# RWKV finish pair by pair with small root tiles, and memory attention's first loads moved into the chunk loop

## The chip, the cores and the metric

One core of one Trainium2 chip runs the whole layer in one launch. The metric is the device time of an execution in microseconds (us). The engines are TensorE (PE), VectorE (DVE), ScalarE (ACT), GpSimd (POOL) and SyncE (SP); SP's queue issues most DMAs.

## The reference, cut to what matters

A decoder layer in float32: a SwiGLU half-step, a mixer of three branches, merged by sigmoid gates and projected, and another SwiGLU half-step; D_MODEL 1024, 1024 tokens. The parts that the change touches:

```python
def rwkv7_mix(p, ...):                      # first branch
    ...
    y = rwkv7_recurrence(r, decay, k, v, -kk, kk * a)   # 8 heads of 64, token by token
    mean = jnp.mean(y, axis=-1, keepdims=True)
    var = jnp.mean(jnp.square(y - mean), axis=-1, keepdims=True)
    y = ((y - mean) * lax.rsqrt(var + RWKV_GN_EPS) * gn_g + gn_b)
    y = y + jnp.sum(r * k * r_k, axis=-1, keepdims=True) * v
    return (y.reshape(B, S, RWKV_WIDTH) * g)            # g = sigmoid(gd) @ g_up

def memory_cross_attention(q, mem_n, w_kv):             # 4 heads of 128, 256 memory tokens
    km, vm = jnp.split(mem_n @ w_kv, 2, axis=-1)
    ...
    s = jnp.einsum('bshd,bmhd->bhsm', q * MEM_HEAD_DIM ** -0.5, km)
    pr = jax.nn.softmax(s, axis=-1)
    o = jnp.einsum('bhsm,bmhd->bshd', pr, vm)

merged = g_a * (y_a @ w_branch[0]) + g_b * (y_b @ w_branch[1]) + g_c * (y_c @ w_branch[2])
```

## The kernel before

Activations lie feature-major: 128 features on the partitions, tokens along the free side. Float32 products are made of three matmuls of 128x128 weights against 512 tokens, out of high and low parts (`mm3`); `operand` splits each weight block on ScalarE (`w_hi`, L300) and VectorE (`w_lo`, L302), ahead of its use.

A planner builds the instruction order of every engine at compile time from priorities and estimated times; on the chip each engine runs its own list in that order and waits on semaphores. `keep_in_program_order` pins the instructions given to it to their order in the text, each engine's among themselves. `issue_after(x)` puts an instruction behind `x` on `x`'s engine. `high_priority` moves work up. Tiles come from pools; a new tile over old memory waits until the old tile has been read. A pool opened with `reuse_waits="tile"` waits tile by tile; the pool `attw` of the attention's small tiles isn't opened so.

The order in the middle of the mixer:

1. `rwkv_chain` runs the recurrence in 16 chunks of 64 tokens; `chunk_fetch` loads the next chunk's operands (`f`, `dinv`). Each chunk has a serial chain of small matmuls (`z`, `y`, `gram`, `bkt`, all in line L1218 or L1258). Matmuls of the two early gates, 10 and 11 (`pgate`, lines 377 to 379), stand between them.
2. Later gates and two branch products form a generator, `filling`; `fill(n, behind)` takes steps of it until n matmuls are covered, behind a given matmul. Most steps hold 6 matmuls, a gate has 48, and what a step takes beyond n counts for the next call.
3. `rwkv_finish` works on 4 pairs of heads, each in two halves of 512 tokens. Per half: GpSimd squares `y` (`ysq`, L1335), ScalarE squares it rounded (`ysq_hi`, L1336), VectorE takes the difference (`ysq_lo`, L1337), two matmuls sum over a head (`var`, L1347), ScalarE takes Ln (L1349) and, once all halves are through, Exp (L1353) over whole pairs: 1 / sqrt. Then per half three VectorE steps with y, gain, bias, bonus (`bo_in`) and the output gate's product (`gup`, L1369), and a store (L1372). `yrs` is one tile of 16 KB per partition.
4. `gate_out` of a gate ends in Tanh on ScalarE (L1483). While the finish is emitted it goes to a list, `held`, which is worked off between the roots and the final steps.
5. `attention` runs 8 memory blocks and 8 window blocks of 128 queries in a software pipeline: scores of block i+1 (`msc`), filling, values of block i-1, turning of block i (`mptr`), filling. `load` of a memory block fetches the queries, `qm`. The keys `km_in` and values `vm_in` are loaded at the start of the attention's section; their pools lie where those of the chain were.

A function's ScalarE table is loaded when the one that is in doesn't hold it; `preload_act_table_set` asks for the one with both Ln and Exp. PSUM has 8 banks of 512 values: 4 under the tag "mm" (`pgate` among them), 4 under "bg" (`var`, `gup`, `msc` among them).

## Time and profile before

| | |
|---|---|
| median of 3 runs | 2264.32 us (2263.44 to 2266.61) |
| the profiled execution | 2261.35 us, span 2259.3 us |
| TensorE busy | 2229.2 us (99%), granted clock 0.998 |
| VectorE, ScalarE, GpSimd busy | 1641.6, 1032.3, 80.1 us |
| DMA | 432.43 MB, 191 GB/s over the span |

Busy times are sums of instructions on an engine. The profile can say for each idle stretch which instruction or DMA ended it (waits), follow the work that ended last back through its releasers (the chain), and give busy times and the granted clock for any window. The chunk loop stands at about 1061 to 1165 us of the span, the finish at 1171 to 1212, the first memory block at 1224.

### The profile page before, as it was taken

How to read it: one execution, taken by the hardware profiler on the slowest of the kernel's cores; microseconds unless marked ns; L12 is line 12 of the kernel's file. 1: busy time of each engine (PE TensorE's matmuls, PEld its weight loads, DVE VectorE, ACT ScalarE, POOL GpSimd, SP SyncE). 2: the span in 40 equal slices, each digit the busy share in tenths (PEclk: the TensorE clock that was granted, in tenths of full speed). 3: DMA queues.
4: the chain of work that ended last, by engine and by line, in shares of the span. 5: the costliest groups of instructions: out<-in, count | busy, mean ns of one | idle time of the engine just before them, and what ended most of it. 6: DMA issues, size and time to landing. Idle time of an engine off the chain costs nothing.

```text
span 2259.3 us, 34577 instructions
## 1 busy us (share of the span) xinstructions
PE 2229.2 (99%) x12304; PEld 1832.0 (81%) x12304; DVE 1641.6 (73%) x2761; ACT 1032.3 (46%) x1935; POOL 80.1 (4%) x154
## 2 busy tenths in 40 slices
PE   8999999999999999999999999999999999999998
PEld 6888888888887788887877887788888888888887
DVE  6988777766698887863656578794898886656576
ACT  6622333454556654444454454444663223345451
POOL 0000000000000011001330000000000000000000
PEclk9999999999999999999999999999999999999999
DMA  8565566686665456455426887564565653347663
GB/s 284 173 204 170 198 210 215 229 289 213 185 217 185 126 148 212 156 166 182 145 86 238 274 277 253 164 223 138 174 210 179 194 187 103 114 165 249 205 194 122
DMA packets 272237, 432.43 MB, mean 191 GB/s; under 512 B 50848, under 2 KB 89760, under 8 KB 271808
## 3 DMA queue, kind: packets, MB, share of 16 engines
q1 hardware_dynamic: 255968, 402.09, 55.0%
q10 hardware_dynamic: 14816, 27.07, 3.5%
q8 instruction: 97, 1.59, 0.3%
q0 software_dynamic: 1280, 1.05, 0.2%
q14 instruction: 76, 0.62, 0.1%
HBM read 292.75 MB, written 136.31 MB: 190 GB/s over the span
## 4 chain that ended last, share of the span: by engine, by line
PE 90%; DVE 4%; DMA 3%; ACT 2%; issue 1%; SPq 0%; ACTq 0%; DVEq 0%
PE px L377 9%; PE px L379 9%; PE px L378 9%; PE po L377 6%; PE po L378 6%; PE po L379 6%; PE pz L377 4%; PE pz L379 4%; PE pz L378 4%; PE pgate L377 2%; PE pgate L378 2%; PE pgate L379 2%; PE pr L377 2%; PE pr L378 2%; PE pr L379 2%; PE pb L377 2%
## 5 line engine op out<-in xcount | busy, mean ns | idle before, releaser
L300 ACT CAST w_hi<-w_raw 128x512 fp32r<-128x512 f32 x608 | 376.1, 620 | 714.5 <-PE px L378 181.3
L302 DVE TENSOR_TENSOR w_lo<-w_raw,w_hi 128x512 fp32r<-128x512 f32 x608 | 417.1, 688 | 193.2 <-ACT w_hi L300 176.9
L377 PE MATMUL po<-u,w_hi 128*128 128x512 f32 (+1 forms) x476 | 180.9, 380 | 0.0
L379 PE MATMUL po<-u,w_lo 128*128 128x512 f32 (+1 forms) x476 | 180.9, 380 | 0.0
L378 PE MATMUL po<-u,w_hi 128*128 128x512 f32 (+1 forms) x476 | 180.9, 380 | 0.0
L377 PE MATMUL px<-u,w_hi 128*128 128x512 f32 x380 | 148.0, 390 | 0.8 <-DVE km L1611 0.8
L377 PE MATMUL pz<-u,w_hi 128*128 128x512 f32 x380 | 148.1, 390 | 0.0
L379 PE MATMUL px<-u,w_lo 128*128 128x512 f32 x380 | 148.0, 389 | 0.0
L378 PE MATMUL px<-u,w_hi 128*128 128x512 f32 x380 | 147.9, 389 | 0.0
L378 PE MATMUL pz<-u,w_hi 128*128 128x512 f32 x380 | 147.8, 389 | 0.0
L379 PE MATMUL pz<-u,w_lo 128*128 128x512 f32 x380 | 147.8, 389 | 0.0
L377 PE MATMUL px<-f,w_hi 128*128 128x512 f32 x352 | 137.1, 390 | 0.1
L379 PE MATMUL px<-f,w_lo 128*128 128x512 f32 x352 | 137.0, 389 | 0.0
L378 PE MATMUL px<-f,w_hi 128*128 128x512 f32 x352 | 137.0, 389 | 0.0
L486 DVE TENSOR_TENSOR u<-hid,u 128x512 fp32r<-128x512 f32 x114 | 78.4, 690 | 49.9 <-ACT u L485 49.1
L378 PEld LDWEIGHTS po<-u,w_hi 128*128 128x128 f32 x476 | 89.5, 188 | 17.0
L379 PEld LDWEIGHTS po<-u,w_lo 128*128 128x128 f32 x476 | 89.5, 188 | 17.0
L377 PEld LDWEIGHTS po<-u,w_hi 128*128 128x128 f32 x476 | 89.5, 188 | 16.9
L377 PE MATMUL pgate<-u,w_hi 128*128 128x512 f32 x256 | 103.1, 403 | 0.0
L485 ACT CAST u<-hid 128x512 fp32r<-128x512 f32 x114 | 70.7, 620 | 68.8 <-DMA hid<-form_d 59.4
L378 PE MATMUL pgate<-u,w_hi 128*128 128x512 f32 x256 | 101.3, 396 | 0.0
L379 PE MATMUL pgate<-u,w_lo 128*128 128x512 f32 x256 | 100.1, 391 | 0.0
(456 smaller groups left out, 5189.4 us busy)
## 6 DMA issues: line engine op xcount, KB each, us to landing
w_raw<-in_ffn_in SPq DMA_DIRECT2D x224, 256.0 KB
hid<-form_d SPq DMA_DIRECT2D x154, 256.0 KB
w_raw<-in_win SPq DMA_DIRECT2D x112, 256.0 KB
form_d<-g SPq DMA_DIRECT2D x88, 256.0 KB
w_raw<-ffn_sum_d SPq DMA_DIRECT2D x88, 256.0 KB
form_d<-h SPq DMA_DIRECT2D x66, 256.0 KB
w_raw<-in_ffn_out SPq DMA_DIRECT2D x66, 256.0 KB
first_d<-first SPq DMA_DIRECT2D x48, 256.0 KB
```

What stands on the lines that cost most here:

```text
L300: self.nc.scalar.copy(hi, x)
L302: self.split_last = self.nc.vector.tensor_tensor(lo, x, hi.bitcast(F32), ALU.subtract)
L377: mm(out, wh, xh, start=first, stop=False, **kw)
L378: mm(out, wh, xl, start=False, stop=False, **kw)
L379: self.last_mm = mm(out, wl, xh, start=False, stop=last, **kw)
L485: self.nc.scalar.copy(hi, x)
L486: self.nc.vector.tensor_tensor(lo, x, hi.bitcast(F32), ALU.subtract)
```

## The change

Root tiles: `yrs` becomes a tag of three tiles of 2 KB, one for each half, with Ln and Exp one after the other. The finish runs pair by pair: variance, filling of `FINISH[1]`, final steps and stores, filling of `FINISH[2]`; the splits for the output gate stand ahead of it. The held gates come after the finish, behind its last Exp, and gate 11's Tanh is pinned in program order. The filling ahead of the attention is cut. `km_in`, `vm_in` and the queries' tiles get a pool of their own, `ahead`, on the right side of SBUF, open from before the chunk loop to the attention's end; keys, values and the first two blocks' queries are loaded in chunks 3, 5, 7 and 8, behind the chunk's fetch (`asked`).

```diff
+FINISH = (16, 6, 10)
 class WindowBlock(Block):
-        self.qs = self.pool.tile([P, 4, P], F32, tag="qs", name="qs", bufs=2)
+        self.qs = self.ahead.tile([P, 4, P], F32, tag="qs", name="qs", bufs=2)
 class MemoryBlock(Block):
-        self.qm = self.pool.tile([P, 4, P], F32, tag="qs", name="qm", bufs=2)
+        self.qm = self.ahead.tile([P, 4, P], F32, tag="qs", name="qm", bufs=2)
 # chunk_fetch
-            S.dma_start(n["d"][q * 64 : q * 64 + 64], inv_d[c, :, q].rearrange("p s t -> s p t"))
+            self.asked = S.dma_start(n["d"][q * 64 : q * 64 + 64], inv_d[c, :, q].rearrange("p s t -> s p t"))
 # rwkv_chain
             nxt = None if last else load(c + 1)
+            if c in beside:
+                with self.tc.issue_after(self.asked.ins):
+                    beside[c]()
 # rwkv_finish
-        rs = pool.tile([P, NPAIR, T], F32, name="yrs", bufs=1)
-        squares = []
+        squares, rs = [], []
         square(0)
         square(1)
-        self.fill(22, self.behind)
-        for i, (p, cols) in enumerate(halves):
-            ps = self.psum("var")
-            for n, x in enumerate(squares[i]):
-                end = keep(nc.tensor.matmul(ps, self.bones_r, x, start=n == 0, stop=n == 1))
-            square(i + 2)
-            keep(S.activation(rs[:, p, cols], ps, ACT.Ln, bias=self.gn_eps, scale=1.0 / C))
-            if i % 2:
-                self.fill(8 if p < NPAIR - 1 else 30, end)
-        for p in range(NPAIR):
-            keep(S.activation(rs[:, p], rs[:, p], ACT.Exp, scale=-0.5))
         for h in (0, 1):
             self.split(self.sg[:, h * TH : (h + 1) * TH], *(x[:, h * TH : (h + 1) * TH] for x in sg))
         self.split(self.g_up, *up)
+        self.fill(FINISH[0], self.behind)
+        for p in range(NPAIR):
+            for h in (0, 1):
+                cols = halves[h][1]
+                ps = self.psum("var")
+                for n, x in enumerate(squares[2 * p + h]):
+                    end = keep(nc.tensor.matmul(ps, self.bones_r, x, start=n == 0, stop=n == 1))
+                square(2 * p + h + 2)
+                rs.append(pool.tile([P, TH], F32, tag="yrs", name="yrs", bufs=3))
+                keep(S.activation(rs[-1], ps, ACT.Ln, bias=self.gn_eps, scale=1.0 / C))
+                root = keep(S.activation(rs[-1], rs[-1], ACT.Exp, scale=-0.5))
+            self.fill(FINISH[1], end)
+            for h in (0, 1):
+                ...
+                r = rs.pop(0)
+                (the three VectorE steps, gup and the store as before)
+            self.fill(FINISH[2], end)
         held, self.held = self.held, None
-        for f in held:
-            f()
-        (the final steps of all halves, self.fill(10, end) after every second)
+        with self.tc.issue_after(root.ins):
+            for f in held:
+                f()
 # gate_out
-            self.nc.scalar.activation(t[:, h * TH : (h + 1) * TH], ps[h], ACT.Tanh, ...)
+            made = self.nc.scalar.activation(t[:, h * TH : (h + 1) * TH], ps[h], ACT.Tanh, ...)
+            if g == GATES_EARLY - 1:
+                self.tc.keep_in_program_order(made)
 # attention
-        blocks[0].load()
-        blocks[1].load()
-        self.fill(50, self.behind)
 # mixer
+            stay = contextlib.ExitStack()
+            ahead = stay.enter_context(tc.tile_pool(reuse_waits="tile", name="ahead", bufs=1, side="right"))
+            km = ahead.tile([P, 4, MEM], F32, name="km_in")
+            vm = ahead.tile([P, 2, 512], F32, name="vm_in")
+            ...
+            beside = {3: lambda: nc.sync.dma_start(km, km_d), 5: lambda: nc.sync.dma_start(vm, vm_d), 7: blocks[0].load, 8: blocks[1].load}
-                self.fill(12, self.solved[-5])
-                self.fill(8, self.solved[-1])
+                self.fill(8, self.solved)
-                km = ap.tile([P, 4, MEM], F32, name="km_in")
-                vm = ap.tile([P, 2, 512], F32, name="vm_in")
-                nc.sync.dma_start(km, km_d)
-                nc.sync.dma_start(vm, vm_d)
```

## Prediction

> **What bounds the kernel now.** I read the page's busy table first, then the waits, then the chain and the engines' timelines around the places that the diff touches. The table says that TensorE is the bound:

> ```profile
> span 2259.3 us, 34577 instructions
> PE 2229.2 (99%) x12304; PEld 1832.0 (81%) x12304; DVE 1641.6 (73%) x2761; ACT 1032.3 (46%) x1935; POOL 80.1 (4%) x154
> ```

> Only 30.1 us of the span are left in which TensorE is idle. The change adds no matmul and takes none out, so it can win only what idles, or runs slowly, where it works. The waits between 1160 and 1230 us (line, releaser, total, times, longest) give that:

> ```profile
> PE msc L101 <- DMA vm_in<-vm_d: 4.3, 1, 4.3
> PE var L1347 <- ACT ysq_hi L1336: 1.2, 1, 1.2
> PE var L1347 <- DVE ysq_lo L1337: 0.5, 2, 0.3
> SPq L191 <- DMA y_d<-yrs: 3.5, 1, 3.5
> ```

> The long one stands where the attention begins. The timelines of SyncE's queue and TensorE, then two steps of the chain, show why:

> ```profile
> 1206.07 5.63 SPq L1372 DMA_DIRECT2D y_d<-yrs  x4
> 1216.04 0.93 SPq L191 DMA_DIRECT2D qm<-att_d  x2
> 1218.03 0.43 SPq L1830 DMA_DIRECT2D vm_in<-vm_d  x1
> 1224.57 3.46 PE L101 MATMUL msc<-km_in,qm 128*128 128x256 f32 x8 [4.28 <-DMA vm_in<-vm_d]
> ...
> 1218.03 6.46 DMA vm_in<-vm_d
> 1224.57 3.46 PE msc L101 x8
> 1237.60 1.73 PE msc L101 x8
> ```

> The query loads stood behind the last store of `yrs`, whose memory they reuse; km and vm stood behind them; TensorE ran out of filling work and waited 4.28 us. The first eight score matmuls then cost 3.46 us, the next eight 1.73: the clock had dropped.

> ```profile
> 1175.60:1185.30 9.70, 7.93 (x32) 5.74 (x31) 5.64 (x7) 9.19 (x14) 6.33 (x6) 1.00 0.08 27
> 1224.50:1228.00 3.50, 3.43 (x9) 2.84 (x10) 0.69 (x1) 0.00 (x0) 0.00 (x0) 0.56 0.61 231
> ```

> In these windows (width, then busy time of PE, PEld, DVE, ACT and POOL, granted clock, DMA share, GB/s) the clock is 1.00 around the three short waits at `var`, which together are 9.70 - 7.93 = 1.77 us, and 0.56 after the long one.

> **The change, part by part.** Times below are of the profiled execution (2261.35 us, 2.05 of it outside the span); the median of the runs shown is 2264.32, 2.97 above, and I carry differences over to it.

> *Loads in the chunk loop.* km, vm and two queries move to chunks 3, 5, 7 and 8, into memory that no `yrs` holds. That takes away the wait (4.28) and the slow clock (3.46 - 1.73 = 1.73): 6.01 us. What do they cost there? SyncE issues four DMAs, each under half a microsecond, behind the chunk's own fetch:

> ```profile
> 1144.30 0.33 SPq L1203 DMA_DIRECT2D f<-pk_d  x1
> 1151.26 0.68 PE L1218 MATMUL y<-center,f 64*64 64x64 f32 x16
> ...
> 1145.00:1148.50 3.50, 3.50 (x55) 3.02 (x50) 2.52 (x8) 2.05 (x5) 0.07 (x1) 1.00 0.73 226
> 1199.00:1212.00 13.00, 13.00 (x59) 10.75 (x58) 12.89 (x21) 2.41 (x4) 0.00 (x0) 1.00 0.84 293
> ```

> A fetch issued at 1144.3 has landed by 1148.5; the first matmul that reads it starts at 1151.26: 2.8 us of cover. The extra 0.52 MB takes 1.8 us at the 293 GB/s of the window from 1199 to 1212, so the cover holds: 0. Were every microsecond of the 1.57 MB exposed it would be 5.4 us; were two fetches late past their cover, about 1. I keep 0 to 1.

> *Table loads.* The last early gate is now pinned ahead of the logarithm's table and the held gate waits for the last root, so Ln, Exp and Square run in one stretch. Before, tanh cut in:

> ```profile
> 1178.89 1.28 ACT L1483 ACT_TABLE_LOAD   x1
> 1180.18 0.69 ACT L1483 ACTIVATE gate<-pgate,half_gb 128x512 f32<-128x512 f32 x1
> 1180.77 0.62 ACT L1336 ACTIVATE ysq_hi<-y 128x512 fp32r<-128x512 f32 x1
> 1181.40 1.28 ACT L1349 ACT_TABLE_LOAD   x1
> ```

> Load and tanh put the square off by 1.9 us, and `var` waited. Six loads of 1.28 us in this stage become two; ScalarE's 5.1 us are worth only the waits, 1.77 us.

> *Fewer fillings.* Each filling step is 6 matmuls. Ahead of attention 12+8+22+8+8+8+30+4x10+50 = 186 become 8+16+4x(6+10) = 88, in whole steps 90. The other 96 run later in attention: 0. Where does less cover show? After the chunk chain ends, TensorE had 18 matmuls before the first `var`, now 12.

> ```profile
> 1170.78 0.68 PE L1218 MATMUL y<-f,sv 64*64 64x64 f32 x16
> 1171.51 0.37 ACT L1269 COPY y<-y 128x256 f32<-128x256 f32 x1 [0.84 <-PE y L1218]
> 1171.89 1.28 ACT L1340 ACT_TABLE_LOAD   x1
> 1173.19 1.15 ACT L1336 ACTIVATE ysq_hi<-y 128x512 fp32r<-128x512 f32 x2
> 1173.85 1.29 DVE L1337 TENSOR_TENSOR ysq_lo<-ysq,ysq_hi 128x512 fp32r<-128x512 f32 x2 [2.46 <-ACT ysq_hi L1336]
> ...
> 1202.58 1.37 PE gup L1369 x6
> ```

> From the end of `y` (1171.4) the two low parts are ready at +3.1 and +3.75 us. Twelve matmuls at 1.37/6 = 0.228 give 2.74, then the high part 0.23: the first low part is 0.2 late, the second another 0.2. New stall 0.4 us (0 if the table load is put ahead of the copy, 0.8 if the queue order is worse).

> *The finish pair by pair.* TensorE per pair: 4 `var` (0.93), 6 filling, 6 `gup` (1.37), 6 or 12 filling: 5.0 to 6.4 us, 24.2 for four. VectorE now has squares and final steps in one stretch:

> ```profile
> 1194.30:1211.00 16.70, 16.70 (x75) 13.82 (x74) 16.51 (x26) 6.02 (x10) 0.00 (x0) 1.00 0.70 241
> 1174.62 2.87 POOL L1335 TENSOR_TENSOR ysq<-y 128x512 f32<-128x512 f32 x2 [1.56 <-DVE ysq_lo L1337]
> 1175.07 1.53 DVE L486 TENSOR_TENSOR g_up<-g_up 128x512 fp32r<-128x512 f32 x1
> L1337 DVE TENSOR_TENSOR ysq_lo<-ysq,ysq_hi 128x512 fp32r<-128x512 f32 x8 | 6.4, 830 | 6.3 <-ACT ysq_hi L1336 6.1 <-PE var L1347 0.2
> ```

> 24 final steps and two weight splits took 16.5 us, so the steps 15.2; six low parts at 0.64 (half of 1.29) add 3.9, three splits 2.0: 21.1 us. GpSimd's squares slow VectorE beside them: 0.2 us each (mean 0.83 against 0.64) to 0.84 (1.53 against 0.69). Six make 1.2 to 5.0: 22.3 to 26.1 us against 24.2. About even. What would make TensorE wait is a `gup` whose PSUM bank VectorE has not freed. Counted from the start of a pair, the roots end at 2.3 and 4.1 us (Square, Ln, Exp, twice, some 0.6 each, as the 1.15 for two squares), the last step some 2.8 to 3.3 later, at 6.9 to 7.4; the next pair's second `gup` needs that bank at 8.0 even after the short pair. Slack 0.6 to 1.1. I take 0.3 us of wait (0 to 3).

> [...]

> *Small root tiles.* A root now lives in one of three tiles until its store has landed. The last store was issued at 1211.4 and the waiting query load left at 1216.04: up to 4.6 us. About 5 us from Ln to the last step and 4.6 for the store, two per pair, in three tiles: 6.4 us per pair against 6.05. So ScalarE's Ln can slip by some 0.4 us per pair. The Square of the next pair's first half stands ahead of it, so `var` does not see it. The held tanh of gate 12 does: it waits for the last root, and gate 14 needs gate 12's two banks. From the start of the fourth pair: root 4.1, table 1.28, two tanh 1.3: 6.7; gate 14 begins after the pair (6.4), the scores (1.73) and gate 13's last 6 (1.37): 9.5. Slack 2.8: 0.

> *First softmax.* Its small tiles lie where the finish's lie and wait for the last store; last step 7.4, lag 0.5, store 4.6: 12.5 us after the start of the fourth pair. The softmax before took from 1226.65 to 1235.27, other work of VectorE included:

> ```profile
> 1226.65 0.69 DVE L202 TENSOR_REDUCE mst<-msc 128x2 f32<-128x512 f32 x1 [4.64 <-PE msc L101]
> 1234.13 1.14 DVE L211 TENSOR_SCALAR mp<-mp,mst 128x256 f32<-128x256 f32 x4
> ```

> So 8.6 more, 21.1; the turning matmuls come at 25.9 (6.4, scores 1.73 twice, 42 and 28 matmuls). Slack 4.8: 0.

> The sum: 6.01 + 1.77 - 0.4 - 0.3 = 7.1 us. Span 2252.2, profiled time 2254.3, against the median **2257.2 us**.

> **The rivals.** *1. The finish becomes VectorE's or ScalarE's* (places: `gup` and `var`). For it: 26.1 against 24.2 us at the upper bound. Against it: the lag falls on steps that nobody waits for until a bank runs out. Price 3 us (1.9 of VectorE and 4 x 0.4 of ScalarE, less 0.6 of slack): 2260.2. In one piece it might also slow the clock, which the trace shows full after 1.2 us of idling and halved after 4.28: then 2261.9. [...]

> *2. The wait moves instead of going.* Only the loads leave the old memory; softmax tiles do not. From 4.8 us later than I reckon the first turning stops TensorE; at 9 us it stops for what `msc` cost, 4.3 + 1.7: gain 1.1, 2263.2. Against it: attention's queue traffic begins later than these stores.

> *3. Slower: the held gate.* SyncE issues in order, and weight loads wait there for their buffers:

> ```profile
> SPq L291 <- DVE w_lo L302: 34.6, 12, 8.3
> SPq L1372 <- DVE yrs L1371: 5.9, 8, 1.5
> ```

> This is of the whole stretch from 1040 to 1230. A store of `yrs` behind one 8.3 us wait lands 8.3 late, the fourth Ln after it too, hence the last root, the tanh and gate 14: 8.3 - 2.8 = 5.5 of waiting, 1.7 of slow clock, gain gone: 2264.4. From there on it decides; two such waits in a row give 13.8 + 1.7: 2272.7. Against it: all eight stores (L1372) waited for VectorE's last step, not behind a load.

> **How the numbers follow.** The forecast 0.66, with its own range 2255 to 2259.5 (7.8 gained with no new wait and 1.5 us of spread between runs, or 4.8); rival 1 0.18; rival 2 0.08; rival 3 0.08, of which 0.03 break even. About 0.2% (4.5 us, below 2259.8) is what a measurement of this kernel can tell. Faster: the forecast and a third of rival 1, 0.72; within: the rest of it, rival 2 and the breaking even, 0.23; slower 0.05. The range takes in rivals 1 and 2: 2253.5 to 2264; rival 3 and the tails stay out.

> **What the profile after would show.** Right: no row of `msc` behind a DMA; the first eight score matmuls at 1.7 to 1.9 us and no window before the tail below clock 1.00; km's and vm's issues between 1080 and 1110, no later chunk; one table load ahead of the first Square and none until the last Exp; TensorE idle about 25 us (30.1 - 6.05 + 0.7). A new wait of some 0.4 us at the first `var`. Wrong: `y` or `gram` waiting for `f` (loads), `gup` for VectorE's last step (rival 1), `mptr` for softmax (rival 2), `pgate` for tanh (rival 3). What would make the forecast wrong is an instruction order on VectorE or SyncE other than the one I assume: the trace before cannot show the new queues.

## The result, and the profile after

The changed kernel takes 2252.8 us (median of 4, 2252.33 to 2256.49) against 2263.88 (2263.07 to 2266.61): a ratio of 0.9949, 95% interval 0.9932 to 0.9967. A second set gave 2254.59 against 2262.51, 0.9958 (0.9946 to 0.9970). Over all its ten executions the median is 2254.1; over the 69 of the kernel before it is 2263.2. The forecast was 2257.2, with a range from 2253.5 to 2264: the change gained some 9 us where 7 were forecast. The first set lies 0.7 us below the range, the second set and the ten together lie in it.

The profiled execution after (2256.49 us, span 2254.8) is the slowest of its ten, the one before (2261.35) among the fastest of its kind; the pair differs by only 4.9. The page's span and busy table after:

```profile
span 2254.8 us, 34592 instructions
PE 2227.1 (99%) x12304; PEld 1830.2 (81%) x12304; DVE 1642.5 (73%) x2761; ACT 1029.6 (46%) x1935; POOL 81.3 (4%) x154
```

TensorE is idle for 27.7 us of this span, and for 26.0 and 26.7 in two later profiles of the same kernel, where the forecast had about 25. Its waits after (line, releaser, total, times, longest) that the forecast names or should have named:

```profile
PE mptr L105 <- ACT mp L208: 3.1, 1, 3.1
PE gup L1368 <- DVE g_up L487: 0.6, 1, 0.6
PE gup L1368 <- DVE yrs L1369: 0.5, 1, 0.5
```

`msc` no longer waits, and `var` is under the rows shown. The timeline after, of TensorE at the first scores, of SyncE's queue, and of ScalarE at the end of the finish:

```profile
1197.21 1.89 PE L102 MATMUL msc<-km_in,qm 128*128 128x256 f32 x8
...
1078.76 0.60 SPq L1815 DMA_DIRECT2D km_in<-km_d  x1
1091.67 0.59 SPq L1815 DMA_DIRECT2D vm_in<-vm_d  x1
...
1195.48 0.63 ACT L1357 ACTIVATE yrs<-yrs 128x512 f32<-128x512 f32 x1
1196.13 1.28 ACT L1484 ACT_TABLE_LOAD   x1
```

The scores start at 1197.2 instead of 1224.6, at full clock, on keys and values loaded over a hundred microseconds earlier, and tanh's table comes after the last Exp. But there is a wait that was not forecast. The timeline of VectorE, ScalarE and TensorE around it:

```profile
1274.15 0.69 DVE L669 TENSOR_TENSOR gin<-gin 128x512 f32<-128x512 f32 x1 [7.39 <-DMA gin<-in_ffn_out]
1274.76 1.28 DVE L203 TENSOR_REDUCE mst<-msc 128x2 f32<-128x512 f32 x2
1276.84 0.47 ACT L208 ACTIVATE mp<-msc,mst 128x256 f32<-128x256 f32 x1 [10.21 <-DVE mst L205]
1277.91 0.66 PE L105 MATMUL mptr<-ident,mp 128*128 128x128 f32 x4 [3.07 <-ACT mp L208]
```

Read upwards: the turning waits 3.07 us for the softmax, that for the maximum, and the maximum stood on VectorE, which keeps its order, behind a sum of feed-forward weights (`gin`) that waited 7.39 us for its load. Behind it the clock halves, as the windows show (width, busy time of the five engines, granted clock, DMA share, GB/s):

```profile
1275.69:1279.10 3.41, 1.19 (x8) 1.06 (x8) 2.66 (x7) 2.27 (x9) 0.00 (x0) 1.00 0.47 179
1279.10:1282.51 3.41, 3.41 (x10) 2.63 (x9) 3.38 (x8) 1.64 (x4) 0.00 (x0) 0.50 0.61 201
```

So this execution paid 3.07 + 3.41/2 = 4.8 us of its own.

### The profile page after: what moved, and what is told of

It is laid out like the page before. It is cut to its first block, busy times and chain, and to the rows that moved or that the text cites. A ratio compares the mean times of both kernels' runs of the same rounds, so it can differ in the third digit from the quotient of the medians.

```text
span 2254.8 us, 34592 instructions
## 1 busy us (share of the span) xinstructions
PE 2227.1 (99%) x12304; PEld 1830.2 (81%) x12304; DVE 1642.5 (73%) x2761; ACT 1029.6 (46%) x1935; POOL 81.3 (4%) x154
## 4 chain that ended last, share of the span: by engine, by line
PE 92%; DVE 4%; DMA 2%; ACT 1%; issue 1%; SPq 0%; ACTq 0%; DVEq 0%
PE px L378 9%; PE px L380 9%; PE px L379 9%; PE po L378 6%; PE po L379 6%; PE po L380 6%; PE pz L378 4%; PE pz L379 4%; PE pz L380 4%; PE pgate L378 2%; PE pgate L379 2%; PE pgate L380 2%; PE pb L378 2%; PE pb L379 2%; PE pb L380 2%; PE pr L378 2%
## 5 line engine op out<-in xcount | busy, mean ns | idle before, releaser
L486 ACT CAST u<-hid 128x512 fp32r<-128x512 f32 x114 | 70.5, 620 | 69.0 <-DMA hid<-form_d 60.1
```

Source lines behind the costliest of these rows:

```text
L486: self.nc.scalar.copy(hi, x)
```

## Experiments

**First: both kernels again, the finish alone, and the softmax ahead of the sums.** The changed kernel again:

> The changed kernel once more, for a second profile of it. Theory A (the edits are worth the 7 to 8 us of the prediction, and the rest is luck of single runs): median 2252 to 2253; the profiled execution shows `mptr` waiting 3 us for `mp` only if its own time is near 2256; where its time is near 2252 that wait is absent. Theory B (that wait is a fixed part of the new order): it is there in this profile too, 3 us with 1.7 us of slow clock behind it, whatever the time.

2254.59 us (five executions, 2251.38 to 2254.93). Its profile (span 2252.9) has this row, and no window below full clock anywhere in the stage (from the chunk loop to the end of the attention):

```profile
PE mptr L105 <- ACT mp L208: 1.3, 2, 1.0
```

So the wait is in the order (theory B is right that it recurs), but its length varies from run to run. A third profile, further down, had 2.1.

The kernel before again:

> The kernel before once more, for a second profile. Theory A (the loads' wait is 4.3 us as in the first profile, with 1.7 us of slow clock; times above 2263 come from elsewhere): `msc` waits 4 to 4.6 us. Theory C (the wait of the late loads varies with the queue, and the first profile had a short one): at a time of 2263 or more `msc` waits 6 us or more, since the stores and loads ahead of it land later.

2263.03 us. Theory A held: `msc` waited 4.2 us, no more than in the first profile, and the longer time comes from elsewhere. (Here and in the next two profiles of this kernel the row names as the end of that wait not `vm_in` but `w_raw<-in_win`, a weight load issued among the same ones, which the scores don't read.) The windows of this run around its `var` waits show where from:

```profile
1181.21:1184.62 3.41, 1.66 (x5) 0.86 (x5) 1.18 (x3) 3.40 (x6) 1.57 (x2) 1.00 0.04 15
1184.62:1188.03 3.41, 3.41 (x9) 2.64 (x8) 1.66 (x2) 3.35 (x5) 0.51 (x1) 0.50 0.00 0
```

The same three short waits that stood at clock 1.00 in the first profile of the kernel before are followed here by 3.41 us at half clock, 1.7 us of lost work. That the short waits halve the clock in some executions is theory L in what follows.

The finish alone: `after` without `beside`, with `km`, `vm` and the queries in the attention's pool and loaded there, and `self.fill(50, self.behind)` back.

> The changed kernel's finish, pair by pair with small root tiles and table loads kept out, but keys, values and first queries loaded at the start of the attention as in the kernel before, behind the last store of `yrs`, with the fifty fillings of that place. Theory A (loads 6 us, finish 1 to 2 us): 2258 to 2260, `msc` waits 4 us or more for a DMA, its first eight matmuls take 3.4 us. Theory C (late loads cost 9 us or more of the 11): 2261 to 2264, `msc` waits 6 us or more. Theory D (the finish is what brought the gain beyond the forecast): 2254 to 2257, with a short `msc` wait.

2256.89 us, ratio 0.9974 (0.9963 to 0.9985). This is not a clean experiment: with that memory layout the scheduler moved the rope angles (L1627 to L1636) onto VectorE inside the chunk loop, where `z`, a step of the chunk's chain, then waits. Waits of this run:

```profile
PE z L1219 <- DVE sv L1311: 2.6, 3, 1.3
PE mptr L105 <- ACT mp L208: 1.3, 1, 1.3
PE msc L102 <- DMA km_in<-km_d: 0.4, 1, 0.4
```

What it does show: with the finish pair by pair the late loads cost 0.4 us, not 4.3. The first query load leaves SyncE at 1205.4 us instead of 1216.0, and the fifty fillings cover most of the rest.

The softmax first:

```
+            with self.k.tc.high_priority(offset=self.k.lead):
                 V.tensor_reduce(st[:, 0, ...], ..., ALU.max)
+        with self.k.tc.high_priority(offset=self.k.lead):
             V.tensor_scalar(st[:, 1], st[:, 0], -scale, None, ALU.mult)
```

> The changed kernel with one addition: VectorE's maximum and negation of each memory block are given priority over the weight sums that are done beside the attention, so that they no longer stand in line behind a sum that waits for its load. Theory A: the wait of `mptr` is absent from the profile, and the median is the changed kernel's or up to 1 us less (2251.5 to 2253), since most executions do not have that wait. Theory B (the wait is in every execution): 4 to 5 us less, 2248.

2254.46 us (2251.1 to 2256.74), 0.9961 (0.9950 to 0.9973): the changed kernel's time, which was 2254.59 in the same set. Its profile (2251.1 us, the fastest of six) had 0.7 us at `mptr`. So theory B, 4 to 5 us less, fell; theory A was right that little is gained, but its 2251.5 to 2253 was missed, and that the wait is gone in every execution isn't shown.

**Second: single parts, tried on the kernel before.** Table loads kept out, nothing else:

```
+            made = self.nc.scalar.activation(t[...], ps[h], ACT.Tanh, ...)
+            if g == GATES_EARLY - 1:
+                self.tc.keep_in_program_order(made)
...
+        with self.tc.issue_after(root.ins):      # root: the last Exp
             for f in held:
                 f()
```

> The kernel before with one part of the change alone: the last early gate's tanh is kept ahead of the logarithm's table load, and the held gates wait for the last root. Theory A (the three short waits at `var` cost their 1.8 us and no more): 1.5 to 2 us less than the kernel before, some 2260.7 against 2262.5, no `var` wait over 0.3 us, the `msc` wait as before. Theory L (the short waits also halve the clock in some executions, by 1.7 us, as in the second profile of the kernel before): 2.5 to 3.5 us less, and the slowest times (over 2265) are gone. Rival: the held tanh now comes so late that `pgate` waits for its bank: no gain, and a `pgate` row among the waits.

2258.23 us against 2263.65, ratio 0.9975 (0.9961 to 0.9988): 5.4 us, more than either theory. Its waits say where the rest is from:

```profile
PE msc L101 <- DMA vm_in<-vm_d: 2.6, 1, 2.6
PE var L1347 <- DVE ysq_lo L1337: 0.4, 1, 0.4
```

The finish ends earlier, so do its stores, and the loads behind them: the `msc` wait is 1.7 us shorter. With the `var` waits (1.75 - 0.4 = 1.4) and the half window behind them (1.7, where an execution has it) that is 4.8 of the 5.4. The two terms that the forecast added are not independent; this edit takes part of the other's.

Which part of the edit does it? The tanh that cut into the finish of the kernel before, at 1180.18 and 1187.99, are the two halves of the first held gate; both early gates had theirs done by 1163.6, ahead of the first table load. So it is the held gate's wait for the last root that counts; pinning the last early gate changes nothing that these profiles show.

More cover, nothing else: `self.fill(50, self.behind)` becomes `self.fill(80, self.behind)`.

> The kernel before with 80 instead of 50 filling matmuls ahead of the attention, everything else as it was: thirty more, 6.8 us of work taken from later. Theory A (the late loads cost the 4.3 us of the wait and 1.7 us of slow clock): 6 us less than the kernel before, some 2256.5 against 2262.5, and no `msc` wait. If later work misses these thirty: less than 6 us, with a new wait in the attention. If the loads cost 9 us or more of the 8 to 11 that the change brought: 2254 or less.

2258.32 us, 0.9974 (0.9965 to 0.9983): 5.3 us less. `msc` no longer waits; the thirty matmuls are missed later, in the products of the branches (`pb`). This run's new wait, and then its windows at and after the `var` waits and at the new one (width, TensorE's busy time, granted clock, DMA share, GB/s):

```profile
PE pb L377 <- DVE u L1743: 3.5, 1, 3.5
```

```profile
1182.74:1186.15 3.41, 1.89 (x7) 1.00 0.00 0
1186.15:1189.56 3.41, 3.41 (x10) 0.50 0.00 0
...
1370.47:1373.88 3.41, 0.34 (x2) 1.00 0.45 170
1373.88:1377.30 3.42, 3.42 (x9) 0.50 0.86 261
```

The halved window behind the `var` waits is there again. The 5.3 us are no clean price of the `msc` wait: the new wait and its half window give 5.2 back in this profile, whose execution (2260.76) is the slowest of the eleven.

Both small edits together:

> The kernel before with both of these small edits: table loads kept out of the finish, and 80 filling matmuls ahead of the attention; the finish is not done pair by pair, the roots stay in one tile, and the loads stay where they were. Theory A (the change's whole gain is the two waits, and its other parts cost and bring nothing): 2253.5 to 2255, the changed kernel's time. If pairing or small roots bring something of their own: 2256 or more. If they cost (the waits at `gup`): 2252 to 2253.

2255.33 us (2255.30 to 2255.89), 0.9962 (0.9950 to 0.9975): 8.3 us, within a microsecond or two of the changed kernel, with 2.8 us of `pb` wait still in it. Against the cover alone the table part is worth 3.0 us: 1.4 of `var` waits and up to 1.7 of clock behind them (0.7 is the shorter `pb` wait, if the profiles stand for the rest).

A place of their own, loads written late: in the changed kernel `beside = {}`, and the four loads stand where the attention begins.

> The changed kernel with keys, values and first queries still in memory of their own, but loaded at the start of the attention, behind the finish's last stores in SyncE's queue, and without the fifty fillings there. Theory A (a place of their own isn't enough: the loads are issued around 1196 us, land some 6 us later, and nothing covers that): `msc` waits 4 to 6 us and the clock halves behind it: 6 to 8 us more than the changed kernel, 2260 to 2262. Rival (what cost time was only the reuse of the `yrs` memory): the loads no longer wait, land at once, `msc` waits less than 2 us: 2254 to 2257.

2252.89 us, 0.9954 (0.9941 to 0.9966): the changed kernel's time. Theory A fell, and the rival was right that `msc` doesn't wait (its 2254 to 2257 was a little too high). The reason is another than it gave, and stands in SyncE's queue:

```profile
1057.81 1.03 SPq L192 DMA_DIRECT2D qm<-att_d  x2
1062.03 0.49 SPq L1835 DMA_DIRECT2D km_in<-km_d  x1
1066.73 0.32 SPq L1836 DMA_DIRECT2D vm_in<-vm_d  x1
```

The planner put the loads where their memory is free, here around the start of the chunk loop (first `z` at 1061.9), and not where the code has them. So whether loads that really run late would do in memory of their own was not tested. What the change bought is the memory of their own; the chunks 3, 5, 7 and 8 are not needed for it.

**Third: taking the new wait away, and taking the table part back.** The sums later: a unit of sums is made only from the eighth call of `unit` on.

> The changed kernel, with the sums of the second feed-forward weights left out of the first seven of the places beside the attention, so that none stands in VectorE's line ahead of a memory block's maximum; they are made later, and none is left out. Theory A (the wait of `mptr` in the changed kernel comes from such a sum that waits for its load, with 1.7 us of slow clock in some executions): no `mptr` wait over 1 us in the profile, and the times above 2255 go: 2251 to 2253. Rival (the sums only move their wait): a `pb` wait of 2 to 4 us later in the attention or behind it, as in the kernel with 80 fillings: 2253 to 2256.

2264.12 us, 1.0004 (0.9996 to 1.0013): the whole gain is gone. `mptr` no longer waits, as theory A said, but the rival was right and too mild. This run's longest wait, and the windows around it:

```profile
PE pb L379 <- DVE gin L1748: 8.4, 4, 4.4
```

```profile
1465.66:1469.07 3.41, 0.00 (x0) 0.00 (x0) 1.12 (x2) 0.20 (x1) 0.00 (x0) 1.00 0.48 190
1469.07:1475.89 6.82, 6.00 (x14) 4.79 (x15) 6.37 (x12) 0.42 (x1) 0.00 (x0) 0.50 0.88 276
```

In the branches the products (`pb`) wait for VectorE's next step, the multiplication by a gate (L1748; its tile is called `gin` too). VectorE itself waited there for loads, between 1440 and 1520 for 10.3 us at sums and for 2.9 at a gate; the longest single wait, 5.3 us for a sum's load, overlaps the longest of TensorE, 4.4 us. TensorE's 8.4 us and two windows at half clock (3.4 us) make 11.8, and less the `mptr` wait that is saved about the 10 us by which this kernel is slower than the changed one.

Table loads let in again:

```
-            if g == GATES_EARLY - 1:
-                self.tc.keep_in_program_order(made)
-        with self.tc.issue_after(root.ins):
-            for f in held:
-                f()
+        for f in held:
+            f()
```

> The changed kernel with its table loads let in again: the last early gate is not pinned and the held gates do not wait for the last root; finish pair by pair, small roots and early loads as changed. Theory A (the table loads cost the `var` waits of the kernel before, 1.8 us): some 2 us more than the changed kernel, 2255 to 2256. Theory L (and these waits halve the clock in some executions): 3 to 3.5 us more, 2256 to 2257.5, and a window with a granted clock below 1 between 1170 and 1195 in the profile, if this execution has it. Rival (the order pair by pair has the slack for them): the same time, 2253 to 2254.5.

2262.54 us, 0.9996 (0.9987 to 1.0005): 8 to 10 us more than the changed kernel in its own sets, worse than all three expectations. The timeline of ScalarE, from tanh's load to the last of the stage:

```profile
1182.45 1.28 ACT L1483 ACT_TABLE_LOAD   x1
1186.07 1.28 ACT L1356 ACT_TABLE_LOAD   x1
1188.07 1.28 ACT L1357 ACT_TABLE_LOAD   x1
...
1201.55 1.28 ACT L1357 ACT_TABLE_LOAD   x1
```

TensorE's waits in this run, and its two windows at half clock:

```profile
PE gup L1368 <- ACT yrs L1356: 2.3, 1, 2.3
PE gup L1368 <- DVE yrs L1369: 1.5, 1, 1.5
PE mptr L105 <- ACT mp L208: 2.1, 1, 2.1
```

```profile
1197.27:1200.68 3.41, 3.41 (x9) 2.63 (x9) 1.74 (x3) 2.76 (x3) 0.00 (x0) 0.50 0.37 132
1238.23:1241.64 3.41, 3.41 (x12) 2.74 (x11) 2.03 (x5) 3.19 (x9) 0.00 (x0) 0.50 0.79 288
```

With root and logarithm next to each other in small tiles, one gate's tanh among them brought a load for each Ln and each Exp after it: with the one ahead of the first Square ten loads in the stage instead of two, 10 us of ScalarE. The gate is again the first held one; the early gates' tanh had ended by 1162 here too, without being pinned. The pair-by-pair finish needs the held gates to wait for the last root; without that its gain is gone.

Sums later and more fillings: `FINISH = (22, 6, 12)` on top of the kernel with the sums later.

> The changed kernel with the sums later and more fillings in the finish: 22 ahead of the first `var` instead of 16, and 12 instead of 10 after each pair. Theory A: the waits at the first `var` (0.5 us) and at `gup` (1.1 us) go too, 1 to 1.6 us less than the kernel with the sums later alone: 2250 to 2251.5. Rival (VectorE is the finish's bound, so that fillings only stand where it would have waited anyway, and what they were is missed later): no less than it.

2270.55 us, 1.0032 (1.0019 to 1.0044). The first `gup` wait is gone, but `pb` waits 6.7 us, and the held gate is late, the end of the chain that rival 3 of the prediction described (that a store stood behind a blocked load, its beginning, isn't shown):

```profile
PE pb L379 <- DVE gin L1748: 6.7, 3, 5.5
PE pgate L379 <- ACT gate L1487: 1.7, 1, 1.7
```

**Fourth: why the gain is larger than the waits of the first profiles.** The table part with twelve more fillings, 62, not 80:

> The kernel before with table loads kept out of the finish, and 62 filling matmuls ahead of the attention instead of 80 (the kernel before has 50): the `msc` wait with the table part alone was 2.6 us, which twelve matmuls of 0.228 us cover. Theory A (the two waits are the whole gain, and the kernel with 80 fillings gave 2.8 us and a halved clock back in its `pb` wait since it had taken more than it needed): no wait over 1 us at `msc` or `pb`, 2251 to 2253. Rival (the `pb` wait has another cause): it stays, 2255.

2256.01 us (2254.47 to 2261.27), 0.9974 (0.9965 to 0.9983). Neither `msc` nor `pb` waits in its profile (2255.38 us) and no window is halved, so theory A was right on the waits and wrong on the time, by 3 us. Some of its executions granted less clock (0.996 and 0.997 in four of eleven) and may have had waits that the profile doesn't have. But the profiled execution is slower than theory A too, by 2.4 us, without such a wait: in the stage TensorE was idle for 2.7 us, no more than in the changed kernel (3.1 and 3.9 in its later profiles), and busy for 452.7 against 450.8. What lengthens the matmuls here is not found.

The kernel before, twice more:

> The kernel before, for its third profile. Theory L (a halved clock after the `var` waits comes in some executions, by where the clock's windows of 3.41 us fall): the waits are 1.7 to 1.8 us again whatever the time; one halved window between 1175 and 1195 in about one execution of three, and then a time 1.7 us longer from there. Theory C (the `msc` wait varies): it is not 4.2 to 4.3 us.

> The kernel before, for its fourth profile, with the same expectations as the third.

2263.18 and 2263.57 us. `msc` waited 4.5 and 4.8 us, and both had the halved window behind `var`. The windows of the last:

```profile
1180.48:1183.89 3.41, 1.70 (x5) 0.97 (x6) 1.18 (x3) 3.40 (x6) 1.70 (x2) 1.00 0.01 4
1183.89:1187.31 3.42, 3.42 (x10) 2.64 (x9) 1.53 (x2) 3.22 (x5) 0.38 (x1) 0.50 0.00 0
```

With the kernel with 80 fillings that makes four profiles of five that have these waits. "One in three" was too low.

The changed kernel once more:

> The changed kernel, for its third profile. Theory A: no wait before `mptr` is the same from run to run; here it is 0.5 to 3 us, and a halved window stands behind it only if it is over 1.5 us. Where it is over 2 us the time is over 2255.

2254.10 us, `mptr` 2.1 us (longest 1.7), no halved window. The wait lies in theory A's range; its last sentence, a time over 2255 where the wait is over 2 us, did not hold if the total is meant.

The windows from the first `z` in the chunk loop to the first matmul of the stage behind the attention (`pw`), TensorE alone. The kernel before, first and fourth profile:

```profile
1064.00:1524.00 460.00, 452.90 (x3666) 1.00 0.64 207
```

```profile
1062.30:1526.30 464.00, 455.66 (x3666) 0.99 0.63 205
```

The changed kernel, second and third profile:

```profile
1063.50:1517.40 453.90, 450.85 (x3666) 1.00 0.64 209
```

```profile
1062.10:1516.80 454.70, 450.81 (x3665) 1.00 0.65 209
```

The same matmuls. The other two profiles before took 463.0 and 462.8, the first after 457.3 with its long `mptr` wait: means of 462.5 and 455.3. Of the 7.1 us between them 3.6 are idle time of TensorE (7.5 against 3.9), 2.4 are work lost in halved windows (3.0 against 0.6), and 1.1 are shorter matmuls. That is less than the 9 us between the medians of all executions, since the first profile after is the slowest of its ten. Behind the stage lie 734.8 to 735.6 us in all seven; in front of it 1062.1 to 1064.0, which the change does not touch.

The mean granted clock of all listed executions fits: of 65 of the kernel before 5 had 0.998, 35 had 0.997, 23 had 0.996 and 2 had 0.995, with median times of 2259.5, 2262.8, 2264.3 and 2266.8; of ten of the changed kernel nine had 0.998 and one 0.997. It doesn't count the windows one by one: a halved window is 1.7 of 2260 us, or 0.0008, but the end of the span, in which TensorE has next to nothing to do, is at half clock too, 7.7 us in the first profile before and 9.7 in the first after, and these 2.0 us alone move the mean by 0.0004. The profile from which I predicted had 0.998:

```profile
core 0: 2259.3 us, clock 0.998
```

It has one halved window ahead of its end, behind `msc`, where the three later profiles of this kernel have two.

## Why the prediction was wrong, point by point

The forecast lay 4.4 us above the first set. Of these 1.1 are the start: I took 2264.32, the median of three runs, where 69 have 2263.2. 1.3 are the first set itself, 2252.8 where the ten have 2254.1. Both come from small samples, and they added up by luck. The other 2.0 are the change: 9.1 gained, 7.1 forecast, and even the most that I had allowed without a new wait was 7.8.

**Loads: right in size, wrong in place.** The `msc` wait and its slow clock, put at 6.01 us, measured 4.2 to 4.8 + 1.7 in the kernel before, and are gone. The cost of 0 beside the chunk chain held (issues at 1078.8 and 1091.7, no wait of `y` or `gram` for `f`). But the chunk loop had no part in it: in memory of their own the loads ran early although the code had them late.

**Table loads: the term that failed.** I put them at the waits' 1.77 us, and read the clock of 1.00 around them as showing that short waits don't slow it. That was one execution. In four profiles of five with these waits a half window follows, so the step that failed is the clock behind the short waits, put at nothing: the term is 1.77 + 1.7, some 3.5 us in such an execution; the table edit measured 3.0 with `msc` covered. In rival 1 I had even priced it ("In one piece it might also slow the clock"), but only for the waits that the change might add, not for those that it removes. The sum with this term is 6.01 + 3.48 - 0.7 = 8.8. Taken from 2263.2, the median of the 69, instead of the 2264.32 of three, it gives 2254.4; the ten executions have 2254.1.

That agreement is partly luck, because smaller terms moved against each other. **Finish and fillings:** the four matmuls of the first `var` took 1.28 us (from 1170.28 to 1171.56) instead of 4 x 0.228: 0.4 us more, as worked out. `gup` waited 1.1 us in all three profiles where I took 0.3 (0 to 3): half of it for the split of `g_up`, which I had counted in VectorE's time but not put ahead of the first `gup`. **Against the gain** stands `mptr`, 1.3 to 3.1 us, which the sum had at 0. **For it** stand 1.1 us that TensorE was busy less (450.8 against 451.9, the halved windows taken off; 451.2 in the first profile before and 452.1 to 452.3 in the other three). What made these matmuls shorter stays open. One possibility is waits too short to show: a matmul of 0.39 us starts every 0.228, so a delay of up to 0.16 us hides in its record.

**Rival 1** (VectorE's finish): VectorE was 92% busy in it, but TensorE waited for it only at `gup`.

```profile
1168.00:1197.20 29.20, 28.09 (x117) 21.30 (x116) 26.90 (x35) 19.06 (x30) 9.79 (x7) 1.00 0.38 126
```

26.90 us of VectorE, weight splits included, where I had 22.3 to 26.1 without them, in a stretch of 29.2 for which I had 27 (2.7 + 24.2). Beside GpSimd's squares six steps of this stretch took 1.52 or 1.53 us, where the same kinds of step took 0.68 to 0.75 without one: 4.9 us more in all, near the top of the 1.2 to 5.0 that I had put down for them.

**Rival 2** came true in kind, not in cause: the wait did move to `mptr`, but the softmax was late for a weight sum's load, not for `yrs`' last store. I had looked at the stores and not at what else stands in VectorE's line in the attention. **Rival 3** did not happen here; the end of its chain, a product that waits for the held tanh, showed in the kernel with more fillings (`pgate`, 1.7 us).

## What to carry to other kernels

One profile shows one throw of the clock: here the same short waits, 1.7 to 1.8 us in all, were followed by 3.41 us at half clock (1.7 us of lost work) in four profiles of five, and the one from which I priced them was the fifth; several profiles tell how often it happens. Two edits that shorten the same chain (a finish and the loads behind its stores) don't add up, so try each alone on the kernel before. A load's place in the code is not its place in time: what held it back here was the memory that it shared. A forecast carried over to a median needs a median of many runs: three were 1.1 us off.

## What the runs showed of the hardware

```profile
1179.82:1183.24 3.42, 2.65 (x11) 1.61 (x9) 0.96 (x2) 3.38 (x5) 2.16 (x2) 1.00 0.23 77
1183.24:1186.65 3.41, 2.41 (x9) 1.79 (x10) 2.25 (x3) 3.41 (x7) 1.09 (x2) 1.00 0.00 0
```

Around 1.5 to 1.7 us both outcomes occur: in the kernel with 80 fillings a window with 1.52 us of idle time (3.41 - 1.89, shown above) was followed by a halved one, and in the second profile of the kernel before one with 1.66, far ahead of the stage, was not (TensorE alone):

```profile
778.43:781.85 3.42, 1.76 (x8) 1.00 0.75 247
781.85:785.26 3.41, 3.41 (x17) 1.00 0.66 153
```

So these profiles show no idle time that separates the two outcomes; the ends of matmuls, from which it is taken, are modelled.
